# An opening copy of 16 x 64 bytes and three early loads at the head of a softmax kernel

## The chip, the cores and the metric

The kernel runs on one core of one Trainium2 chip. The metric is the time of one execution on the device in microseconds (us); lower is better. Beside timed runs there is a profile of one execution; its span, from the first to the last instruction, is some 1.8 us shorter than the time on the device. "Faster" or "slower" is said only from 2% on.

Names used below: SP issues the loads, ACT computes the exponentials and issues the stores, DVE takes row maxima and scales, POOL does almost nothing. "Load 2" is the second load in the kernel's order (1.31 MB; the profile's views write it as 1280.0 KB of 1024 bytes). A "packet" is one contiguous piece that one of the 16 transfer engines moves.

## The reference

```python
x = np.random.randn(16, 1024, 512).astype(np.float32)

def reference(x):
    x_max = np.max(x, axis=-1, keepdims=True)
    exp_x = np.exp(x - x_max)
    return (exp_x / np.sum(exp_x, axis=-1, keepdims=True)).astype(np.float32)
```

A softmax over rows of 512 numbers: 33.55 MB in, 33.55 MB out.

## The kernel before

The rows are cut into ten chunks. A chunk of R has R rows on each of 128 partitions; so load packets are R x 2 KB long. The first eight loads do not depend on computed data; even so, the trace shows loads 6 to 8 issued only at 4.5, 7.5 and 24.3 us, after waits on earlier transfers. The two last loads reuse the place of stored chunks.

```python
CHUNKS = [
    (3, 0), (5, 3), (8, 8), (16, 16), (16, 32), (16, 48), (16, 64), (16, 80), (16, 0), (16, 16),
]
EARLY = 8
AFTER_STORE = {2: [8], 3: [9]}
GROUP = 8
AT_HEAD = {mybir.EngineType.SP: 1}

def loads_at_the_head(nc):
    main, body = nc.main_func.blocks[0], nc.main_func.blocks[1]
    for engine, count in AT_HEAD.items():
        loads = [ ... the first `count` transfers of that engine ... ]
        barrier = ... position of the engine's first InstDrain in main ...
        for load in loads:
            body.instructions.remove(load)
        main.instructions[barrier:barrier] = loads
```

All engines meet at an opening barrier before the body starts. The function above moves the first load ahead of SP's part of that barrier. The body, per group of up to 8 rows:

```python
# rowmax: one reduction on DVE for the group
nc.vector.reduce_max(out=shift[g], in_=place[k][:, a:b, :], axis=AX, negate=True)
# exps: one activation on ACT per row, with the row's sum
nc.scalar.activation(out=place[k][:, r, :], in_=place[k][:, r, :], func=EXP,
                     bias=shift[g][...], scale=1.0, accum_out=sums[g][...])
# scale: reciprocal and one multiplication per row on DVE, then the store
nc.scalar.dma_start(out=dst[k][:, since:b, :], in_=place[k][:, since:b, :])
```

Of the kernel before, what the change touches and what calls it, by code (L numbers as in the profile page):

```python
# [1 line left out]

# [4 lines left out]

F32 = mybir.dt.float32
EXP = mybir.ActivationFunctionType.Exp
AX = mybir.AxisListType.X  # L10


CHUNKS = [
    (3, 0), (5, 3), (8, 8), (16, 16), (16, 32), (16, 48), (16, 64), (16, 80), (16, 0), (16, 16),
]
SBUF_ROWS = 96
# [6 lines that stand above are left out]
FINISH_BEFORE = (1, 2, 3)  # L23

STORE_ROWS = {3: 8, 4: 8, 5: 8}

ON_ACT = ()

AT_HEAD = {mybir.EngineType.SP: 1}



def loads_at_the_head(nc):

    main, body = nc.main_func.blocks[0], nc.main_func.blocks[1]
    for engine, count in AT_HEAD.items():
        loads = [
            i
            for i in body.instructions
            if i.engine == engine and type(i).__name__ == "InstDMACopy"  # L40
        ][:count]
        barrier = next(
            n
            for n, i in enumerate(main.instructions)
            if i.engine == engine and type(i).__name__ == "InstDrain"
# [6 lines that stand above are left out]
@with_exitstack  # L52
def kernel(
    ctx: ExitStack,
    tc: tile.TileContext,
    x: bass.AP,
    out: bass.AP,
):
    nc = tc.nc
    nc.at_finalize(loads_at_the_head)  # L60
    P = nc.NUM_PARTITIONS

    x_flat = x.flatten_outer_dims()
    out_flat = out.flatten_outer_dims()
    n, d = x_flat.shape
    assert n == P * sum(R for R, _ in CHUNKS)


    src, dst, at = [], [], 0
    for R, _ in CHUNKS:  # L70
        for flat, views in ((x_flat, src), (out_flat, dst)):
            part = flat[at : at + P * R, :]
            views.append(part.rearrange("(p r) d -> p r d", r=R))
        at += P * R

    data = ctx.enter_context(tc.tile_pool(name="data", bufs=1))
    stats = ctx.enter_context(tc.tile_pool(name="stats", bufs=4))
    held = data.tile([P, SBUF_ROWS, d], F32, name="held")
    place = [held[:, s : s + R, :] for R, s in CHUNKS]


    groups = []
    for k, (R, _) in enumerate(CHUNKS):
        m = max(1, round(R / GROUP))
        cuts = [R * i // m for i in range(m + 1)]
        since = 0
        for a, b in zip(cuts, cuts[1:]):
            ends = b == R or b - since >= STORE_ROWS.get(k, R)
            groups.append((k, a, b, since if ends else None))
            since = b if ends else since  # L90
    shift = [None] * len(groups)
    sums = [None] * len(groups)

    def load(k):
        queue = nc.scalar if k in ON_ACT else nc.sync
        queue.dma_start(out=place[k], in_=src[k])

    def rowmax(g):
        k, a, b, _ = groups[g]
        shift[g] = stats.tile([P, b - a], F32, name="shift", tag="shift")  # L100
        nc.vector.reduce_max(  # L101
            out=shift[g], in_=place[k][:, a:b, :], axis=AX, negate=True
        )

    def exps(g):
        k, a, b, _ = groups[g]
        sums[g] = stats.tile([P, b - a], F32, name="sums", tag="sums")
        for r in range(a, b):
            nc.scalar.activation(  # L109
                out=place[k][:, r, :],  # L110
                in_=place[k][:, r, :],
                func=EXP,
                bias=shift[g][:, r - a : r - a + 1],
                scale=1.0,
                accum_out=sums[g][:, r - a : r - a + 1],
            )

    def scale(g):
        k, a, b, since = groups[g]
        recip = stats.tile([P, b - a], F32, name="recip", tag="recip")  # L120
        nc.vector.reciprocal(out=recip, in_=sums[g])  # L121
        for r in range(a, b):
            nc.vector.tensor_scalar_mul(  # L123
                out=place[k][:, r, :],
                in0=place[k][:, r, :],
                scalar1=recip[:, r - a : r - a + 1],
            )
        if since is not None:
            nc.scalar.dma_start(
                out=dst[k][:, since:b, :], in_=place[k][:, since:b, :]  # L130
            )
        if b == CHUNKS[k][0]:
            for later in AFTER_STORE.get(k, ()):
                load(later)

    with tc.manual_schedule():
        for k in range(EARLY):
            load(k)
        waiting = None
        for g, (k, a, _, _) in enumerate(groups):  # L140
            if waiting is not None and a == 0 and k in FINISH_BEFORE:
                scale(waiting)
                waiting = None
            rowmax(g)
            exps(g)
            if waiting is not None:
                scale(waiting)
            waiting = g
        scale(waiting)


# [1 line left out]
_INS = ['x']  # L153
_OUTS = [((16, 1024, 512), 'float32')]


# [23 lines left out]
```

## Time and profile before

| | before |
|---|---|
| median time, 4 runs | 161.56 us (161.53 to 161.69) |
| span of the profiled run | 159.7 us |
| DVE, ACT busy | 78%, 58% |
| bytes moved | 67.1 MB, 432 GB/s in the middle of the span |
| loads 1, 2, 3, 4 issued at | 0.00, 0.78, 1.16, 1.63 us |
| SP passes the opening barrier | 0.70 us |
| first store issued, its first packet | 10.04, 13.88 us |

The prediction below shows the page's lines and how to read them. In a view by stretches the columns are the stretch, its length, busy time and count of DVE, ACT and POOL, the TensorE clock, the DMA share and GB/s.

The view of transfers by size gives load 2's time from issue to landing (last column, us):

```profile
held<-in_x_dram SPq DMA_DIRECT2D x1, 1280.0 KB, 6.7
```

Issued at 0.78, it landed at 7.5 us.

### The profile page before, as it was taken

What the parts mean: (1) busy time and instruction counts of PE and PEld (TensorE: products, weight loads), DVE (VectorE), ACT (ScalarE), POOL (GpSimd) and SP (SyncE); (2) the same over time, 40 slices, a digit from 0 to 9 for tenths busy, and PEclk for the clock granted to TensorE, in tenths of its full rate; (3) what the DMA queues carried; (4) which work ended last, traced back from release to release, by engine and by line L of the source; (5) the groups of instructions that cost most, each with busy time, mean ns of one, the idle gap of its engine ahead of it and who ended that gap; (6) DMA issues with size and microseconds to landing.
All of it is one profiled execution on the core that took longest, in us unless ns stands there. A gap on an engine that the chain in (4) does not pass through costs nothing.

```text
span 159.7 us, 521 instructions
## 1 busy us (share of the span) xinstructions
DVE 123.9 (78%) x162; ACT 93.3 (58%) x257; POOL 0.2 (0%) x4
## 2 busy tenths in 40 slices
DVE  0481870799699999999999999999999999762000
ACT  0718129208994959595868677686859595930000
POOL 0000000000000000000000000000000000000000
DMA  7999999899999999999999999999999999999993
GB/s 269 433 464 411 389 447 446 383 412 466 402 441 431 460 435 396 439 418 468 427 414 439 414 484 427 396 447 402 435 439 476 418 402 468 443 402 468 427 410 164
DMA packets 3315, 67.13 MB, mean 420 GB/s; under 512 B 368, under 2 KB 368, under 8 KB 624
## 3 DMA queue, kind: packets, MB, share of 16 engines
q1 hardware_dynamic: 1440, 33.56, 49.5%
q10 hardware_dynamic: 1872, 33.56, 48.9%
q14 instruction: 3, 0.02, 0.0%
HBM read 33.55 MB, written 33.55 MB: 420 GB/s over the span
## 4 chain that ended last, share of the span: by engine, by line
DVE 70%; ACT 14%; issue 3%; DMA 3%; DVEq 0%; ACTq 0%
DVE shift L101 38%; DVE held L123 30%; ACT held L109 14%; DMA held<-in_x_dram 3%; DVE recip L121 2%; DVEq L175 0%; ACTq L109 0%
## 5 line engine op out<-in xcount | busy, mean ns | idle before, releaser
L109 ACT ACTIVATE held<-held,shift 128x512 f32<-128x512 f32 x128 | 90.5, 709 | 43.4 <-DVE shift L101 33.2
L101 DVE TENSOR_REDUCE shift<-held 128x8 f32<-128x4096 f32 (+2 forms) x17 | 70.6, 4161 | 4.5 <-DMA held<-in_x_dram 4.5
L123 DVE TENSOR_SCALAR held<-held,recip 128x512 f32<-128x512 f32 x128 | 52.2, 481 | 0.6
L109 ACT ACTIVATION_READ_ACCUMULATOR held<-held,shift 128x1 f32 x128 | 24.0, 187 | 0.0
L121 DVE RECIPROCAL recip<-sums 128x8 f32<-128x8 f32 (+2 forms) x17 | 3.3, 193 | 15.8 <-ACT held L109 15.8
L109 ACT ACT_TABLE_LOAD x1 | 1.3, 1283 | 4.5 <-DMA held<-in_x_dram 4.5
L164 POOL MEMSET const-bfloat16-1.0<- 128x1 bf16 x1 | 0.1, 102 | 0.0
L164 POOL MEMSET const-uint8-127<- 128x1 uint8 x1 | 0.1, 102 | 0.0
L164 POOL MEMSET const-float32-1.0<- 128x1 f32 x1 | 0.1, 99 | 0.0
L164 POOL MEMSET const-float32-0.0<- 128x1 f32 x1 | 0.1, 98 | 0.2 <-issue 0.2
## 6 DMA issues: line engine op xcount, KB each, us to landing
held<-in_x_dram SPq DMA_DIRECT2D x7, 4096.0 KB, 41.8
out_dram<-held ACTq DMA_DIRECT2D x4, 4096.0 KB, 21.0
out_dram<-held ACTq DMA_DIRECT2D x7, 2048.0 KB, 35.5
held<-in_x_dram SPq DMA_DIRECT2D x1, 2048.0 KB, 11.3
held<-in_x_dram SPq DMA_DIRECT2D x1, 1280.0 KB, 6.7
out_dram<-held ACTq DMA_DIRECT2D x1, 1280.0 KB, 20.0
held<-in_x_dram SPq DMA_DIRECT2D x1, 768.0 KB, 4.5
out_dram<-held ACTq DMA_DIRECT2D x1, 768.0 KB, 15.7
```

What stands on the lines that cost most here:

```text
L101: nc.vector.reduce_max(out=shift[g], in_=place[k][:, a:b, :], axis=AX, negate=True)
L109: nc.scalar.activation(out=place[k][:, r, :], in_=place[k][:, r, :], func=EXP, bias=shift[g][:, r - a : r - a + 1], scale=1.0, accum_out=s ...
L121: nc.vector.reciprocal(out=recip, in_=sums[g])
L123: nc.vector.tensor_scalar_mul(out=place[k][:, r, :], in0=place[k][:, r, :], scalar1=recip[:, r - a : r - a + 1],)
L164: nc = _bacc.Bacc("TRN2", target_bir_lowering=False, num_devices=1)
```

## The change

ACT issues a tiny copy from input to output ahead of the barrier (16 pieces of 64 bytes). The author's reason is not recorded; the evident one is to use ACT's transfer queue once before it matters. SP issues three loads ahead of the barrier in place of one. The first store waits for the opening copy, because it overwrites its bytes.

```diff
-AT_HEAD = {mybir.EngineType.SP: 1}
+AT_HEAD = {mybir.EngineType.Activation: 1, mybir.EngineType.SP: 3}
...
-        m = max(1, round(R / GROUP))
+        m = -(-R // GROUP)
...
-            nc.scalar.dma_start(
+            store = nc.scalar.dma_start(
                 out=dst[k][:, since:b, :], in_=place[k][:, since:b, :]
             )
+            if k == 0:
+                tc.add_manual_dep(store.ins, opening.ins.name, ...)
...
     with tc.manual_schedule():
+        step = P * CHUNKS[0][0] // 16
+        opening = nc.scalar.dma_start(
+            out=out_flat[: 16 * step : step, :16], in_=x_flat[: 16 * step : step, :16]
+        )
         for k in range(EARLY):
             load(k)
```

The second hunk gives the same groups for chunks of 3, 5, 8 and 16 rows. What remains are the two parts in the title.

More of the change, by code (lines that the diff above doesn't have):

```diff
@@ L25, with transfers_at_the_head @@
 STORE_ROWS = {3: 8, 4: 8, 5: 8}
-ON_ACT = ()
-AT_HEAD = {mybir.EngineType.SP: 1}
-def loads_at_the_head(nc):
+AT_HEAD = {mybir.EngineType.Activation: 1, mybir.EngineType.SP: 3}
+def transfers_at_the_head(nc):
     main, body = nc.main_func.blocks[0], nc.main_func.blocks[1]
@@ L59 @@
     nc = tc.nc
-    nc.at_finalize(loads_at_the_head)
+    nc.at_finalize(transfers_at_the_head)
     P = nc.NUM_PARTITIONS
@@ L94, in load @@
     def load(k):
-        queue = nc.scalar if k in ON_ACT else nc.sync
-        queue.dma_start(out=place[k], in_=src[k])
+        nc.sync.dma_start(out=place[k], in_=src[k])
     def rowmax(g):
@@ L128, in scale @@
         if since is not None:
-            nc.scalar.dma_start(
+            store = nc.scalar.dma_start(
                 out=dst[k][:, since:b, :], in_=place[k][:, since:b, :]
             )
+            if k == 0:
+                tc.add_manual_dep(
+                    store.ins,
+                    opening.ins.name,
+                    mybir.DependencyInfo(
+                        mybir.DependencyClass.Sync, mybir.DependencyReason.DATA
+                    ),
+                    reason="overwrites what the opening transfer wrote",
+                )
         if b == CHUNKS[k][0]:
@@ L136 @@
     with tc.manual_schedule():
+        step = P * CHUNKS[0][0] // 16
+        opening = nc.scalar.dma_start(
+            out=out_flat[: 16 * step : step, :16], in_=x_flat[: 16 * step : step, :16]
+        )
         for k in range(EARLY):
```

## The prediction

> **What bounds the kernel now.** I read the page first: parts 1 and 2 (who is busy, and when), then part 3 (the DMA queues).
>
> ```profile
> span 159.7 us, 521 instructions
> ## 1 busy us (share of the span) xinstructions
> DVE 123.9 (78%) x162; ACT 93.3 (58%) x257; POOL 0.2 (0%) x4
> ...
> DMA  7999999899999999999999999999999999999993
> GB/s 269 433 464 411 389 447 446 383 412 466 402 441 431 460 435 396 439 418 468 427 414 439 414 484 427 396 447 402 435 439 476 418 402 468 443 402 468 427 410 164
> ...
> HBM read 33.55 MB, written 33.55 MB: 420 GB/s over the span
> ```
>
> No compute engine is full: DVE 78%, ACT 58%. The DMA row is full from the second slice to the last but one, and only the two end slices are not. The chain of waits on the page follows DVE and ACT, but the last store is issued at 144.8 us and the span ends at 159.7, so the chain does not name the limit. The transfer engines do: 67.1 MB must pass through them, and compute only decides in what order.
>
> Next I cut the span into stretches and read DMA share and GB/s (the last two columns). A packet counts wholly where it starts, so a short stretch is uncertain: 16 packets of 32 KB are 0.52 MB, which is 1.2 us of traffic. I trust stretches of 20 us to a per cent, and those of 4 or 5 us only roughly.
>
> ```profile
> 0.00:1.00 1.00, 0.00 (x0) 0.00 (x0) 0.20 (x4) 1.00 0.00 0
> 1.00:5.00 4.00, 0.52 (x1) 0.47 (x1) 0.00 (x0) 1.00 1.01 378
> 5.00:10.00 5.00, 2.67 (x6) 3.04 (x7) 0.00 (x0) 1.00 0.99 418
> 10.00:15.00 5.00, 2.74 (x2) 2.23 (x7) 0.00 (x0) 1.00 1.09 438
> 15.00:20.00 5.00, 3.53 (x7) 1.41 (x4) 0.00 (x0) 1.00 0.96 413
> 20.00:40.00 20.00, 14.15 (x12) 9.01 (x25) 0.00 (x0) 1.00 1.01 429
> 40.00:60.00 20.00, 18.40 (x27) 15.71 (x45) 0.00 (x0) 1.00 1.01 433
> ...
> 140.00:155.00 15.00, 3.46 (x9) 1.21 (x4) 0.00 (x0) 1.00 1.02 439
> 155.00:158.60 3.60, 0.00 (x0) 0.00 (x0) 0.00 (x0) 1.00 0.57 246
> 158.60:159.70 1.10, 0.00 (x0) 0.00 (x0) 0.00 (x0) 1.00 0.00 0
> ```
>
> From 40 to 140 us the five stretches of 20 us show 433, 432, 432, 435 and 429, mean 432 GB/s. That makes a **budget**: 67.13 MB at 432 GB/s is 155.4 us; 1.0 us before the first byte; 1.1 us after the last; together 157.5 of 159.7. The remaining 2.2 us lie in the slow start (1 to 5 us at 378 in place of 432: 4 x 54/432 = 0.5 us), in 5 to 20 us (mean 423: 15 x 9/432 = 0.3 us), some 0.1 us in 20 to 40, and the ragged end (155 to 158.6 at 246: 1.5 us), less 0.2 us that 140 to 155 is above the mean. A change at the head can reach only the first 1.0 us, the 0.5 and the 0.3. **Even all of that, 1.8 us, is 1.1% of 161.57 us.**
>
> **Where those 0.3 us are.** I went from stretches to the trace's records of single DMA packets. A 32 KB load packet takes 1.213 us (median). In 12 to 14 us, just before the store queue's first packet appears at 13.88 us, 18 load packets take 1.34 to 1.61 us instead. Their excess over 1.213, added up and divided by 16 engines, is 0.26 us; with the 2 us on each side 0.35 us. The first store was issued at 10.04 us, so its queue needed 3.8 us for a first packet. Before the later stores' first packets (25.6, 38.6, 53.1 us) the same sum is 0.1 us or less in any 2 us around them. So the first use of ACT's transfer queue seems to disturb each engine by a quarter of a microsecond, once. For SP's queue, the first 8 us hold 0.5 us of such excess.
>
> **What the Trainium skill says.** (1) "DMA: Bandwidth & Descriptors", section "Where 436 GB/s comes from": 16 ports give 435 GB/s at most. The trace agrees: 432 in the steady part. (2) The same page, "Issuing engines are not separate DMA queues": transfers issued by SP and ACT run on the same 16 engines, and several issuers only save sequencer time. The 432 GB/s stays the same whether one queue runs (110 to 140 us, stores only) or both. (3) The same page, "Queues, rings and completion order": each queue has its own ring on every engine, and an engine alternates between rings that have work. The trace shows that: between 14 and 16 us the 6 KB store packets and the 32 KB load packets alternate. (4) The same page's "Specifications": below 512 B an engine does a read-modify-write. The trace of this kernel has no data packet so small. No page that I found says that a ring's first use costs anything; the 0.26 us is my reading of this trace alone.
>
> **The change part by part.**
> *Opening transfer.* It adds 16 pieces of 64 bytes, 1 KB, on ACT's queue before the opening barrier. Issue: 0.34 to 0.375 us, from the kernel's own store issues, on an ACT that does nothing before 4.5 us: free. On the engines: one 64-byte packet each, plus a completion write; the 4-byte completion packets of this trace take 0.009 us each. With an HBM read and a small write I allow 0.05 us per engine (an estimate). If first use of the ring costs 0.26 us, it is paid here instead, in the time when the engines are idle (the first load byte moves at 1.02 us) or ramping. Gain: between 0 (the stall is merely moved onto the first load) and 0.3 us. I take 0.25.
> *The first store's wait on the opening.* The opening should have landed by about 4 us (the 768 KB first load lands at 4.5); the first store is issued at 10.04. Slack 6 us: free.
> *Three loads at the head.* Now load 1 issues at 0.00, the barrier passes, loads 2 and 3 issue at 0.78 and 1.16 us. After: about 0.37 and 0.70 us (issue times 0.371 and 0.327 us), so 0.4 us earlier. But load 2's first packet moves at 3.38 and load 3's at 6.43 us, when the one before has drained: hidden, gain 0. Against it, SP reaches the barrier 0.33 + 0.42 = 0.75 us later (about 1.45 instead of 0.70). The first compute instruction waits until 4.48 for the first load; slack 3.0 us: cost 0.
> *The grouping line* gives the same groups for 3, 5, 8 and 16 rows: no effect.
> Sum: -0.25 + 0.05 = **-0.20 us**, on 161.57: 161.37; I say 161.35.
>
> **Rivals.** A: *nothing at all.* If the packets slowed because load packets and the first store's reads from SBUF collide, or the opening's stall lands on the first load, the time stays 161.5 to 161.7. For: a first load packet takes up to 0.78 us in place of 0.234 already, so the head has no spare room after 1.02 us. B: *the opening delays the first load.* The two issues share the 16 engines, and a small HBM-to-HBM copy in front could push every packet back by its latency; as transfers are the bound, this adds in full: 161.8 to 162.2. For: the budget has no slack. Against: 1 KB is little, and ACT and SP issue at the same time. C: *the added transfer shifts which semaphores are reused.* SP already waits for earlier transfers before some loads:
>
> ```profile
> SPq L96 <- DMA out_dram<-held: 57.3, 4, 14.5
> SPq L96 <- DMA held<-in_x_dram: 20.7, 3, 16.4
> ```
>
> One transfer more may make a load or a store wait on another predecessor. Against: load 8, issued at 24.3 us, starts moving only at 65.2; the backlog hides microseconds of change. It would hurt only if ACT sat on a store until the queues ran dry; the last store is issued at 144.77 us and starts to move at 147.65, so 2.9 us of slack remain there. D: *a larger gain.* If the slow start of loads (0.5 us) and the latency of 1.0 us also shrank, because an earlier write wakes the path, 160.6 would be possible; nothing in the profile speaks for it.
>
> **Range and chances.** The three timed runs lie within 0.16 us. My own theory gives 161.2 to 161.5, A 161.5 to 161.7, B up to 162.2, D down to 160.6. I give my theory 0.5, A 0.3, B 0.1, the others the rest: 8 in 10 lie in 160.9 to 161.8. Two per cent is 3.2 us; the gain side has 1.8 us in reach at all, the loss side needs a starved queue.
>
> **What would show each step right or wrong.** Right: the store queue's first data packet follows the first store's issue by clearly less than 3.8 us; the load packets before it stay at 1.21 us; steady rate 432; first load byte still at about 1.0 us and first landing at about 4.5; loads 2 and 3 issued at 0.4 and 0.7 us with their packets moving no earlier. Wrong: the slow packets are still there before the first store (rival A, collision), or have moved to 1 to 4 us and the first landing is later (A or B), or a stretch in the middle with GB/s well under 430 (C). The prediction would fail by much only if the transfer engines ran idle somewhere in the middle.

## More of the kernel before

One more view of the kernel before matters later, so it stands here: three stretches of the head.

```profile
1.00:3.00 2.00, 0.00 (x0) 0.00 (x0) 0.00 (x0) 1.00 0.96 326
3.00:5.00 2.00, 0.52 (x1) 0.47 (x1) 0.00 (x0) 1.00 1.06 431
5.00:8.00 3.00, 1.23 (x1) 2.55 (x6) 0.00 (x0) 1.00 1.02 429
```

Load 2's first packet starts at 3.12 us, while the last packets of load 1 run until 4.10, and from 3 us on the rate is the full 430: load 2 follows load 1 without a gap.

## The result, and the profile after

| | before | after |
|---|---|---|
| median time, 4 runs each | 161.56 us | 161.57 us (161.51 to 161.66) |
| span of the profiled run | 159.7 us | 159.9 us |
| loads 1, 2, 3, 4 issued at | 0.00, 0.78, 1.16, 1.63 us | 0.00, 0.42, 0.89, 1.93 us |
| SP passes the opening barrier | 0.70 us | 1.85 us |
| load 2 landed | 7.5 us | 7.5 us |
| first store issued, its first packet | 10.04, 13.88 us | 9.99, 13.79 us |

The ratio is 1.000, with a 95% interval from 0.9982 to 1.0017. Ratios here are the mean time of one kernel's fast runs over that of the other's fast runs of the same rounds, so they are not quite the ratio of the medians quoted.

The page of the changed kernel:

```profile
span 159.9 us, 523 instructions
...
DVE 123.9 (78%) x162; ACT 93.3 (58%) x257; POOL 0.2 (0%) x4
...
DMA  7999899899999999999999999999999999999993
...
HBM read 33.56 MB, written 33.56 MB: 420 GB/s over the span
```

Nothing has moved: the same busy times, the same full DMA row. The first microsecond in order of time shows the two parts of the change:

```profile
0.00 1.52 SPq L93 DMA_DIRECT2D held<-in_x_dram  x3
0.12 0.65 ACTq L146 DMA_DIRECT2D out_dram<-in_x_dram  x1
```

The three loads take 1.52 us to issue and the opening 0.65 us. Alone, ACT's store issues take 0.34 us. Loads 2 and 3 are issued 0.36 and 0.27 us earlier than before. Load 4 is issued 0.30 us later. The three stretches of the head, and load 2 from issue to landing:

```profile
1.00:3.00 2.00, 0.00 (x0) 0.00 (x0) 0.00 (x0) 1.00 0.91 319
3.00:5.00 2.00, 0.58 (x1) 0.53 (x1) 0.00 (x0) 1.00 1.06 430
5.00:8.00 3.00, 1.18 (x1) 2.54 (x6) 0.00 (x0) 1.00 1.03 438
```

```profile
held<-in_x_dram SPq DMA_DIRECT2D x1, 1280.0 KB, 7.1
```

Load 2 went out at 0.42 and took 7.1 us where it took 6.7, so it landed at the same 7.5 us. Its first packet started at 3.20 us (3.12 before): the earlier issue became a longer wait in the queue.

### The profile page after: what moved, and what is told of

Same layout as the page of the kernel before. It is cut to its first block, busy times and chain, and to the rows that moved or that the text cites. A ratio compares the mean times of both kernels' runs of the same rounds, so it can differ in the third digit from the quotient of the medians.

```text
span 159.9 us, 523 instructions
## 1 busy us (share of the span) xinstructions
DVE 123.9 (78%) x162; ACT 93.3 (58%) x257; POOL 0.2 (0%) x4
## 4 chain that ended last, share of the span: by engine, by line
DVE 70%; ACT 14%; issue 3%; DMA 3%; DVEq 0%; ACTq 0%
DVE shift L98 38%; DVE held L120 30%; ACT held L106 14%; DMA held<-in_x_dram 3%; DVE recip L118 2%; DVEq L187 0%; ACTq L106 0%
```

## The experiments

Twelve kernels ran, all with correct results. They ran on two chips and were less quiet than the runs of the result. The kernel before went from 161.52 to 162.95 us in 12 runs on the first and from 161.57 to 162.99 in 11 on the second. So a ratio against before has an interval of about 0.3% either way, and I also compare lowest and highest times. Eight kernels ran on the first of these chips; late_barrier, open_body, before_again and after_more ran on the second.

The theory at the start (T): transfers are the bound, the opening costs nothing on the engines, and the slow load packets ahead of the first store belong to that store and not to the first use of ACT's queue. The rival R1: the opening gains 0.2 us and the three loads lose 0.2 us.

### Is it the transfers that bound the time?

**half_max.** DVE's maximum over half the columns. Softmax does not change by it.

```diff
-            out=shift[g], in_=place[k][:, a:b, :], axis=AX, negate=True
+            out=shift[g], in_=place[k][:, a:b, : d // 2], axis=AX, negate=True
```

> The row maximum is taken over half the columns (softmax does not change by it, up to rounding), which takes about 35 us from DVE. Theory T (transfers are the bound): 161.5 us, ratio 1.000 within 0.2%. Rival R3 (the DVE chain of the page, 70% of the span, is the bound): far less, 130 us or so.

Measured: 161.40 to 161.52 us in 4 runs, ratio 0.9965 (0.9927 to 1.0003).

```profile
span 159.7 us, 522 instructions
...
DVE 90.8 (57%) x162; ACT 92.6 (58%) x257; POOL 0.2 (0%) x4
```

DVE lost 33 us of work, and the best time moved by 0.1 us (from 161.52). The chain that the page follows back through DVE is not the bound.

**big_open.** The opening copies the whole first chunk.

```diff
-            out=out_flat[: 16 * step : step, :16], in_=x_flat[: 16 * step : step, :16]
+            out=out_flat[: 16 * step].rearrange("(p r) d -> p (r d)", p=P),
+            in_=x_flat[: 16 * step].rearrange("(p r) d -> p (r d)", p=P),
```

> The opening copies the whole first chunk, 786 KB, from input to output (overwritten by the first store, so the result stays right). T: every byte the engines move costs, 786 KB at 432 GB/s is 1.82 us, so 163.4 us (ratio 1.011), unless the HBM-to-HBM copy runs slower than that. If the bound were compute, or the head had room for it: 161.6 to 162. Of the slow packets at 12 to 14 us: gone here if they belong to the first heavy use of ACT's queue, since the queue has then moved 48 KB on each engine; still there if they belong to the first store from SBUF or to load 4's start.

Measured: 163.38 to 164.38 us, ratio 1.011 (1.0073 to 1.0147). From lowest to lowest, 163.38 less 161.52, it is 1.86 us for the 1.82 expected. Added bytes cost their full time, even at the head. The slow packets at 12 to 16 us were still there (0.20 us per engine).

### Does the first use of ACT's queue cost anything?

For each 2 us the excess of packets over their usual length is added up and divided by 16 engines. At 12 to 16 us it is 0.28 us before and 0.22 us after: the opening did not remove it.

**late_store.** The first chunk is stored when the second has been scaled.

```diff
+        if k == 1:
+            store_0()          # the first chunk's store, with its wait on the opening
-        if since is not None:
+        if since is not None and k > 0:
```

> The first chunk is stored only after the second is scaled, at about 18.7 us in place of 10.0. If the slow load packets at 12 to 14 us belong to the first store's arrival they move to about 21 us. If they belong to the start of load 4 (its first 32 KB packets begin at 11.3 us) they stay at 12 to 14 us. Time 161.5 to 161.7 either way.

Measured: 161.75 us, one run. The program order let ACT issue the store at 12.88 us and not at 18.7 as I had expected. Its first packet came at 16.74 us, 3.9 us later. The excess at 12 to 14 us was gone and stood at 16 to 20 us (0.42 us per engine). So the slow packets stand around the first store's first packet (in before most start ahead of it, at 12.0 to 13.7 us), and not at the start of load 4 (11.2 us).

**split_load.** Load 4 in four pieces, with packets of 8 KB around the first store.

```diff
-        nc.sync.dma_start(out=place[k], in_=src[k])
+        pieces = 4 if k == 3 else 1
+        rows = CHUNKS[k][0] // pieces
+        for a in range(0, rows * pieces, rows):
+            nc.sync.dma_start(out=place[k][:, a : a + rows, :], in_=src[k][:, a : a + rows, :])
```

> Load 4 is issued as four loads of 4 rows, so the load packets around the first store are of 8 KB in place of 32 KB. If a new queue waits behind a fixed number of packets, the first store's first packet comes within 2 us of its issue in place of 3.8; if it is a fixed time, 3 us or more. The slow packets: if their excess is per packet (0.2 us each), more packets give a longer dip. Time 161.5 to 161.8.

Measured: 162.07 us, one run. The first store's first packet came at 14.34, which is 4.3 us after its issue. The wait is therefore not a fixed number of packets. In 10 to 16 us the excess was 0.82 us per engine, in 76 slow packets, of which 73 were of 8 KB. More packets, more loss. The times of these two runs, and of the next, lie 0.05 to 0.27 us above what I had named; with one run each, on a chip where before itself scatters by 1.4 us, that says nothing.

**sbuf_open.** The opening stores 64 bytes of each partition from SBUF, just after the barrier.

```diff
-AT_HEAD = {mybir.EngineType.Activation: 1, mybir.EngineType.SP: 3}
+AT_HEAD = {mybir.EngineType.SP: 3}
...
+        small = data.tile([P, 16], F32, name="small")
+        nc.gpsimd.memset(small, 0.0)
         opening = nc.scalar.dma_start(
-            out=out_flat[: 16 * step : step, :16], in_=x_flat[: 16 * step : step, :16]
+            out=out_flat[: P * CHUNKS[0][0] : CHUNKS[0][0], :16], in_=small
```

> The opening is a store of 64 bytes of each partition of a small zeroed tile in SBUF to output rows of the first chunk, issued just after the barrier. If the first store from SBUF is what slows the load packets at 12 to 14 us, the excess there (0.19 us per engine in the changed kernel) goes below 0.08; if the opening has nothing to do with it, it stays at 0.15 to 0.3. Time 161.4 to 161.7.

Measured: 161.78 us, one run; 0.23 us of excess at 12 to 16 us. So the first store from SBUF is not it either. With big_open, three kinds of first use left the slow packets in place. The first-use theory of the prediction has fallen; why load packets slow down around the first heavy store stays open.

### The two parts alone

**loads_only**, three loads at the head without the opening; **open_only**, the opening with one load at the head; **after_again**, the changed kernel.

```diff
 # loads_only, against before
-AT_HEAD = {mybir.EngineType.SP: 1}
+AT_HEAD = {mybir.EngineType.SP: 3}
 # open_only, against after
-AT_HEAD = {mybir.EngineType.Activation: 1, mybir.EngineType.SP: 3}
+AT_HEAD = {mybir.EngineType.Activation: 1, mybir.EngineType.SP: 1}
```

> Three loads at the head of SP alone, without the opening. T: 161.55 us, ratio 1.000 within 0.1%; loads 2 and 3 issued at about 0.4 and 0.8 us, their packets no earlier than 3.4 and 6.4. R1: 161.75 us, ratio 1.0012, with the first byte or the barrier later.

> The opening transfer alone, with one load at the head of SP as before. T: 161.55 us, ratio 1.000 within 0.1%, slow load packets still there at 12 to 14 us. R1: 161.35 us, ratio 0.9988, and the slow packets gone.

> The changed kernel once more, with more rounds, to narrow the interval. Theory T (transfers are the bound; the opening costs each engine two packets of 0.01 us, the head of SP hides what the three loads gain): ratio 1.000, within 0.1%. Rival R1 (the opening gains about 0.2 us and the three loads at the head lose about as much, so the two cancel): also 1.000 here. My prediction's first-use gain alone: 0.9988.

| same chip, same rounds | lowest | median | highest | ratio to before (interval) |
|---|---|---|---|---|
| before, 11 runs | 161.52 | 162.19 | 162.95 | |
| loads_only, 6 runs | 161.50 | 161.61 | 161.74 | 0.9974 (0.9945 to 1.0003) |
| open_only, 6 runs | 162.05 | 162.49 | 162.85 | 1.0030 (1.0001 to 1.0059) |
| after_again, 6 runs | 161.50 | 162.06 | 162.88 | 1.0004 (0.9971 to 1.0037) |

This is the reverse of R1 and not what T expected. Against before, from which it differs by the opening alone, open_only **costs** 0.3% or 0.5 us (0.02 to 0.96 us by the interval). Against loads_only it is 0.9 us slower (162.49 less 161.61; the two ranges do not touch), but there the number of early loads differs too. On these chips some executions of before have the same loss (see The scatter), which makes the first figure the smaller one. The profile of open_only (162.57 us) shows where:

```profile
1.00:3.00 2.00, 0.00 (x0) 0.00 (x0) 0.00 (x0) 1.00 0.96 332
3.00:5.00 2.00, 0.44 (x1) 0.39 (x1) 0.00 (x0) 1.00 0.97 254
5.00:8.00 3.00, 1.31 (x1) 2.54 (x6) 0.00 (x0) 1.00 1.00 395
```

```profile
held<-in_x_dram SPq DMA_DIRECT2D x1, 1280.0 KB, 7.0
```

In 3 to 5 us the rate is 254 in place of 431, although the engines count as busy (0.97). This is called the gap below. Worked out against 432: 2 x 178/432 + 3 x 37/432 = 1.1 us lost. Load 2 was issued at 1.42 us, since ACT held the barrier until 1.34 (0.63 us of issue, then 0.39 us in the drain before the barrier, which took 0.01 in before), and landed at 8.4 us, 0.9 us later than in before and after. Thirteen of its 128 packets took more than 0.8 us (0.385 is usual); in the profiles of before, after and loads_only none did. The queue did not start late: load 2's first packet is at 3.23 us, and 11 of the 13 slow ones start by 3.9 us. In loads_only the same stretches are at full rate, with load 2 issued at 0.42:

```profile
3.00:5.00 2.00, 0.63 (x1) 0.58 (x1) 0.00 (x0) 1.00 1.05 439
5.00:8.00 3.00, 1.12 (x1) 2.54 (x6) 0.00 (x0) 1.00 1.02 432
```

### A late second load, or the opening itself?

New theory L: the loss comes from load 2 going out late, whatever holds it. Rival O: the opening's packets themselves disturb the loads.

**late_barrier** (no opening; POOL clears a spare tile before the barrier) and **open_body** (the opening after the barrier, one load at the head).

```diff
 # late_barrier, against before
-AT_HEAD = {mybir.EngineType.SP: 1}
+AT_HEAD = {mybir.EngineType.SP: 1, mybir.EngineType.Pool: 1}   # and memsets may be moved
+        spare = data.tile([P, 1024], F32, name="spare")
+        nc.gpsimd.memset(spare, 0.0)
 # open_body, against after
-AT_HEAD = {mybir.EngineType.Activation: 1, mybir.EngineType.SP: 3}
+AT_HEAD = {mybir.EngineType.SP: 1}
```

> The kernel before, without an opening; POOL clears a spare tile before the barrier, so that load 2 goes out at 1.3 to 1.6 us. Theory L: 162.3 to 162.8 us and load packets of 1 us and more at 3 to 4 us, as in the run with the opening alone. Rival O: 161.5 to 161.7, GB/s in 3 to 5 us at 430.

> The opening is issued by ACT just after the barrier in place of before it, with one load at the head, so that load 2 goes out at about 0.8 us as before. Theory L (the opening alone cost 1 us because it held the barrier and load 2 went out at 1.42 us): the loss is gone, 161.5 to 161.8, GB/s in 3 to 5 us back above 400. Rival O (the opening's small packets among the loads cost it themselves): 162.3 to 162.8 and GB/s in 3 to 5 us below 300.

late_barrier: 162.74 to 163.45 us, ratio 1.0069 (1.0040 to 1.0097), with no opening at all. Load 2 went out at 1.63 us.

```profile
3.00:5.00 2.00, 0.48 (x1) 0.43 (x1) 0.00 (x0) 1.00 0.92 289
5.00:8.00 3.00, 1.27 (x1) 2.54 (x6) 0.00 (x0) 1.00 1.04 398
```

```profile
held<-in_x_dram SPq DMA_DIRECT2D x1, 1280.0 KB, 8.5
```

The same gap in the same place (seven packets above 0.8 us), and load 2 landed at 10.1 us. The memset that held the barrier had ended at 1.3 us, well before the gap. Against 432 the two stretches lose 0.9 us, about half of the 1.9 by which this span exceeds that of before; the last data end at 160.4 us in place of 158.5, and how the rest is lost is not shown.

open_body, with load 2 at 0.78 as before: 161.52 to 162.58 us, ratio 1.000 (0.9966 to 1.0033). It missed the 161.5 to 161.8 that L named, but it scatters as before does on that chip. Its profiled run took 162.31 us and shows no rate below 300, which O had named:

```profile
3.00:5.00 2.00, 0.65 (x1) 0.60 (x1) 0.00 (x0) 1.00 1.00 402
5.00:8.00 3.00, 1.11 (x1) 2.54 (x6) 0.00 (x0) 1.00 1.03 418
```

The interval of open_body alone would still leave room for the 0.3% of open_only. What speaks against O are the traces: late_barrier makes the gap without an opening, and in after the opening's packets start at 3.19 us, among the loads as in open_only (3.15), with 430 GB/s in that stretch. So L is supported and O is not. A late barrier by itself is not the cause either. It is latest in after (1.85 us; 1.55 in late_barrier, 1.34 in open_only), where loads 2 and 3 are already out and the stretch runs at 430. Loads 2 and 3 always moved together in these runs; which of the two matters is not separated, nor why 1.42 us is too late in a queue whose load 1 still moves packets until 4.2 us.

### The scatter

**before_again** and **after_more**: the two kernels unchanged, on the second chip.

> The kernel before once more: on one chip its runs went from 161.5 to 162.95. If load 2 at 0.78 us is on the edge (theory L), a run above 162 shows less GB/s in 3 to 5 us; if the extra time comes from elsewhere, that stretch stays at 430 and another one is lower. On a quiet chip: 161.5 to 161.7 and nothing to see.

> The changed kernel once more, to see whether its runs scatter where those of before do. Theory L: three loads at the head cover the late barrier, ratio 1.000 within 0.2% on a quiet chip; a run above 162 then needs another cause, and its profile shows in which stretch.

before_again: 161.49 to 162.94, ratio 1.0008 (0.9973 to 1.0043). Its profiled run took 162.22 us, and so shows one of the longer executions of the very same program:

```profile
3.00:5.00 2.00, 0.61 (x1) 0.56 (x1) 0.00 (x0) 1.00 0.83 313
5.00:8.00 3.00, 1.15 (x1) 2.54 (x6) 0.00 (x0) 1.00 1.03 364
```

The same stretch, the same gap (four packets of load 2 above 0.8 us), with load 2 at 0.77 us as always in this kernel. In this execution load 2 at 0.77 us met the gap; in the first profile, at 0.78, it did not. after_more: 161.49 to 162.93, ratio 0.9988 (0.9953 to 1.0022). Its profiled run was a quick one (161.49), with 387 GB/s in 3 to 5 us and two packets of load 2 above 0.8 us, so what lengthens some executions of the changed kernel was not caught. An early load 2 does not always prevent slow packets. Five of its 12 runs on the two noisy chips were above 162 us. loads_only had none in 6, but half_max, with the same head as the changed kernel, had none in 4. Whether loads_only is really steadier than the changed kernel stays open; its ratio to before still includes 1.

Two things support L beyond the single profiles. Over both noisy chips, the share of runs above 162 us rises with the time at which the profiles show load 2 issued: 5 of 18 at 0.42 us (loads_only, after_again, after_more), 20 of 35 at 0.78 (before, before_again, open_body), 6 of 6 at 1.42 (open_only) and 6 of 6 at 1.63 (late_barrier). And in the profiled runs of these kernels the span goes with load 2's landing: 159.7 to 159.9 us where it landed at 7.4 to 7.8, 160.4 to 160.8 where at 8.4 to 9.1 (before_again, open_only, open_body), 161.6 at 10.1. So a late issue makes the gap more likely, and is not its only condition.

## Why the prediction was right or wrong

The measured 161.57 us lies in the range of 160.9 to 161.8. The time moved by 0.01 us, where two per cent would be 3.2. The named gain of 0.20 us did not come. My own theory, given 0.5, named 161.2 to 161.5 and failed; the range held because it also took in rival A, given 0.3. That the number fits is luck as far as my theory goes.

- **The bound.** Right. half_max took 33 us from DVE for 0.1 us of time, and big_open paid 1.86 us for bytes worth 1.82.
- **First use of the ring: 0.25 us gained.** This is the step that failed, and what the prediction called its own theory. The excess was 0.28 us before and 0.22 after, the first packet came 3.8 us after the issue both times, and a full 786 KB through the queue did not remove it. Nor was the opening paid for in idle time: its first packet moved at 3.19 us, 3.1 us after its issue began, among the packets of load 2. Rival A, nothing at all, is what happened in the quiet runs of the result.
- **Opening on the engines: 0.05 us.** Right in kind, even too high: its packets took 0.011 us each, with 0.009 for the completions.
- **The first store's wait on the opening: free.** Right. The opening landed at 4.5 us, 4.4 after its issue, and the store was issued at 9.99.
- **Opening's issue: "free".** Wrong taken alone. It took 0.65 us and not 0.34, and held the barrier that SP's second load stands behind. In open_only that cost 0.5 us against before, and 0.9 us against loads_only. I had asked what the barrier delays on the compute engines and found 3.0 us of slack; the load behind it had none.
- **Three loads at the head: "hidden, gain 0".** The sum is right: landing at 7.5 us in both. The first packets I misread: in the trace of before load 2's starts at 3.12 us and not 3.38, load 3's at 6.25 and not 6.43. The slack that I took from this, between issue and first packet (0.78 to 3.12, 2.3 us), is not slack: 0.6 us more delay opened a gap. What the three loads do is take loads 2 and 3 out from behind a barrier that the opening makes late. The parts of the change belong together: in the profiles of after and after_again the gap of open_only is gone. The times lean the same way (162.06 against 162.49 us), but their ranges overlap.
- **The barrier at 1.45 us.** Measured 1.85: SP's second and third issue took 0.42 and 0.63 us, not the 0.33 and 0.42 that I had put. It had no effect on compute: DVE waited for load 1 until 4.42 us.
- **Rivals B and C.** B had a delay from the opening, though by its data and on load 1; the actual one was by its issue and on load 2, and the other half of the change covered it. Of C nothing was seen: 432 GB/s from 40 to 140 us again. Nor of D: the first load byte still moved at 1.00 us.

## What to carry to other kernels

When transfers are the bound, the compute engines' slack says nothing about the loads: before delaying a barrier, ask which transfer issue stands behind it. The time between a load's issue and its first packet is not slack: in open_only load 2 had 1.8 us of it and still lost time. Here, getting loads 2 and 3 out ahead of the barrier made such losses rarer, though it did not end them. A stretch with a low rate and a few packets several times their usual length is the sign, even where the DMA share looks full; test each half of such a change alone, since two halves may cancel.

## What the Trainium skill lacked or had wrong

- "DMA: Bandwidth & Descriptors", "Issuing engines are not separate DMA queues", says that several issuers only save issue time, "usually small relative to the DMA itself". Here the issue of the copy from HBM to HBM took 0.63 to 0.67 us wherever it stood, with 1 KB or 786 KB, against 0.34 for most stores and 0.37 for sbuf_open's small store from SBUF. SP's third load took 0.63 us to issue in after and 0.43 in loads_only; why is not shown, as load 4 took 0.60 in before without any copy. A load 2 issued 0.6 us later behind such an issue cost 0.5 us of the whole time against before.
- The same page, "Specifications", gives a first-byte latency of about 0.6 us for transfers issued by SP and ACT. It does not say from where it counts. Load 1's first packet came 1.0 us after its issue began and 0.65 us after it ended (the issue took 0.37), which agrees if the end is meant. A first store on engines full of loads took 3.5 to 4.5 us from the start of its issue to its first packet.
- No page that I found says that load packets slow down around the first heavy store's first packet: 0.2 to 0.4 us per engine with 32 KB packets, 0.82 us with 8 KB packets.
- No page that I found says how late a second load may be issued behind the first: the rate in 3 to 5 us was 430 to 440 GB/s in three profiles with load 2 at 0.42 us and 387 in a fourth, 431, 402 and 313 in three at 0.78, 254 at 1.42 and 289 at 1.63.
